# Hybrid S5 and attention block on one Trainium2 core: chunk outputs in pairs, Toeplitz blocks by way of DRAM

## Chip, cores and metric

One core of a Trainium2 chip runs the whole layer as one program. The metric is the device time in microseconds; before, it is 681.32 us (median of 3 runs, 681.21 to 681.42).

## What is computed

One decoder layer on 512 tokens of width 1024 in float32: RMSNorm, one input projection `h @ w_in` of 9216 columns, an S5 state-space branch, a dilated attention branch, gates, and an output projection. The change concerns the S5 branch. Cut to it, the reference is

```python
def chunk_step(carry, u_c):                       # u: 64 groups of 16 channels, 64 complex states each
    bu = einsum('blgp,gnp->blgn', u_c, bb)        # input to states (complex)
    h  = scan(h[t] = a * h[t-1] + bu[t])          # diagonal, per state
    y  = einsum('blgn,gpn->blgp', h_re, c_re) - einsum('blgn,gpn->blgp', h_im, c_im)
y = y + d_skip * u
g = gelu(y)
return g * sigmoid(g @ w_glu)
```

## The kernel before

Float32 accuracy comes from three passes in fp32r: each operand is split into a high and a low part (ACT writes the high part, DVE the low one: lines 234 and 236 for weights), and `mm3` (line 144) issues three matmuls of up to 512 columns. A projection unit of 128 output columns is 24 such matmuls, in the trace `pj`. Weights come through SP's queue into two raw tiles (line 220) and are converted two units ahead of their use.

The order of PE is written out by hand: every matmul and transpose is issued after the one before it (`issue_after`, lines 62 to 74). A running list of units (u, za, zs, v0, v, rs, ra; lines 886 to 889) is the filler, and `events` (lines 874 to 884) says before which group of six matmuls a piece of the S5 branch is put. One group is two k-steps of `mm3`, a unit of the filler four groups. The other engines' orders, and SP's, are picked by the framework's scheduler from a simulated timeline, subject to the data and to priorities that follow the program's order. `W0` = 16, `K0B` = 49, `V0B` = 74 and `Y0` = 88 are places in the count of groups.

The S5 branch takes time in steps of eight tokens (T = 8, 64 columns of steps), and has these pieces:

- `w_unit`, `x_unit` (lines 369 and 387): inputs to states for 8 groups, eight times, into `Xs`.
- the scan (lines 665 to 720) on DVE, in 11 portions put at every fourth group from W0+26. `tables_last` holds it behind the last coefficient operation traced so far (`coefs[0]`, line 356).
- `ca_load`, `ca_turn`, `ca_coef` (lines 736 to 766): for one of eight units j (8 groups of 16 channels each), C is loaded, turned on PE (`cps`), copied out by ACT into one of two scratch tiles `p3`, and multiplied with powers of A on DVE (12 operations, lines 354 to 356) into one of three buffers `ab[j % 3]`.
- `m_unit` (line 768): CA times B on PE (`kps`) gives the first block row of a Toeplitz matrix for each group; ACT copies 8 pieces of 16 rows to `kt`, POOL adds the diagonal of d_skip (`dg`), and POOL issues eight transfers from SBUF to SBUF (line 785), each shifted by 16 columns, into M, one of three buffers `Mb` that were zeroed once (`clear_m`).
- `y_unit` (line 788): M times inputs (`yps <- dd,uss`) plus CA times states (`yps <- ab,Xs`), 48 matmuls in the program and 96 in the trace; ACT copies to `ysb`.
- `g_unit` (line 814): `ysb` turned back on PE (`yT`), GELU on ACT and DVE, split into `gT_hi` and `gT_lo`, the inputs of the GLU matmuls that follow the filler.

`chunk(j)` (line 851) strings these together: turn of ysb j-1, turn of C for j+3, y of j, coefficients of j+3, M of j+2, loads of u for j+2 and of C for j+4. It is put at Y0 + (11 j + 1)//3, so at groups 88, 92, 95, 99, 103, 106, 110 and 114, and the last turn at 116. Three turns of C, at W0+16, W0+19 and W0+22, lie ahead of the scan; M for units 0 and 1 is made at K0B.

PSUM: projection tiles take banks 0 to 2 in turn, everything else (`bank`) banks 3 to 7 in turn. Tiles named `t2k` share six buffers.

## Time and profile before

| | before |
|---|---|
| median of 3 runs | 681.32 us |
| the profiled execution | 681.33 us |
| its span, first to last instruction | 679.3 us |
| PE, PEld busy | 671.1, 565.1 us |
| DVE, ACT, POOL busy | 465.5, 322.1, 119.9 us |
| SP's queue (hardware): packets, MB | 134872, 78.93 |
| POOL's queue (software): packets, MB | 2048, 2.36 |
| granted TensorE clock, mean | 0.999 |

Times in the views are microseconds from the start of the span. Groups of instructions are told by line, engine, operation and tiles (out <- in); line 69 and line 74 are the helpers through which all matmuls and transposes go, so PE is read by tile names. One row of a timeline is: start, duration, engine, line, operation, tiles, shapes, count, and in brackets how long the engine had been idle and what released it. A fp32 matmul shows as two instructions. In a list of waits the three numbers are: us in total, times, the longest. Matmuls are pipelined, so what one costs is read from start to start. The stretches of the chunks lie between 177 and 244 us.

### The profile page before, as it was taken

The page shows a single profiled execution, that of the slowest core. Times are in us where ns is not written, and L with a number is a line of the kernel's source. Part 1 is how long each engine was busy: PE and PEld are TensorE (multiplying, and loading weights), DVE is VectorE, ACT ScalarE, POOL GpSimd, SP SyncE. Part 2 cuts the span into 40 slices and gives each one's busy share as a digit, 9 for nine tenths or more (in the row PEclk, how much of TensorE's full clock was granted, in tenths as well). Part 3 has the DMA queues.
Part 4 walks back from the last instruction along what each step waited for, and adds up shares of the span by engine and source line. Part 5 has one row for each costly group of instructions (what it writes and reads, how often), then busy time and mean ns, then how long its engine had stood idle before and what let it go on. Part 6 is the DMA issues. An engine that isn't in the chain of part 4 may idle for free.

```text
span 679.3 us, 12710 instructions
## 1 busy us (share of the span) xinstructions
PE 671.1 (99%) x4826; PEld 565.1 (83%) x4826; DVE 465.5 (69%) x981; ACT 322.1 (47%) x675; POOL 119.9 (18%) x274
## 2 busy tenths in 40 slices
PE   8999999999999999999999999999999999999997
PEld 7988878889888888888889888888888888888886
DVE  7879879999788466653238777558675856667531
ACT  5454543423377664431244673556455745733210
POOL 1021000500255529610000030012001200120000
PEclk9999999999999999999999999999999999999999
DMA  9656524643556653563333422222322223237231
GB/s 293 122 140 166 130 70 114 173 144 108 154 117 158 154 155 117 182 202 108 94 93 94 140 63 83 58 79 63 94 67 74 78 63 94 94 131 288 94 124 62
DMA packets 137236, 82.13 MB, mean 121 GB/s; under 512 B 32720, under 2 KB 125656, under 8 KB 137048
## 3 DMA queue, kind: packets, MB, share of 16 engines
q1 hardware_dynamic: 134872, 78.93, 39.4%
q0 software_dynamic: 2048, 2.36, 2.2%
q8 instruction: 38, 0.62, 0.4%
q14 instruction: 22, 0.18, 0.1%
q10 hardware_dynamic: 256, 0.04, 0.0%
HBM read 68.46 MB, written 10.49 MB: 116 GB/s over the span
## 4 chain that ended last, share of the span: by engine, by line
PE 75%; issue 10%; DVE 6%; POOL 4%; ACT 2%; DMA 2%; SPq 0%; POOLq 0%; DVEq 0%; ACTq 0%
PE pj L69 63%; POOL dd L785 3%; PE sps L69 2%; PE ot L69 2%; PE ptp L74 2%; PE qtp L74 1%; DVE w_lo L236 1%; PE xps L69 1%; PE wps L74 1%; ACT w_hi L234 1%; DMA x_all<-in_x_dram 1%; DVE scn L686 1%; DMA dg<-in_d_skip_dram 1%; PE yps L69 1%; POOL kt L781 1%
## 5 line engine op out<-in xcount | busy, mean ns | idle before, releaser
L234 ACT ACTIVATE w_hi<-w_raw 128x1024 fp32r<-128x1024 f32 x96 | 101.7, 1060 | 170.8 <-PE pj L69 142.4
L236 DVE TENSOR_TENSOR w_lo<-w_raw,w_hi 128x1024 fp32r<-128x1024 f32 x96 | 120.2, 1253 | 76.0 <-ACT w_hi L234 75.4
L69 PE MATMUL pj<-hT_hi,w_hi 128*128 128x512 f32 (+1 forms) x344 | 131.8, 385 | 0.0
L69 PE MATMUL pj<-hT_lo,w_hi 128*128 128x512 f32 (+1 forms) x344 | 128.3, 376 | 0.0
L69 PE MATMUL pj<-hT_hi,w_lo 128*128 128x512 f32 (+1 forms) x344 | 126.6, 375 | 0.0
L69 PE MATMUL pj<-w_hi,hT_hi 128*128 128x512 f32 (+1 forms) x288 | 108.7, 377 | 0.0
L69 PE MATMUL pj<-w_hi,hT_lo 128*128 128x512 f32 (+1 forms) x288 | 105.6, 367 | 0.0
L69 PE MATMUL pj<-w_lo,hT_hi 128*128 128x512 f32 (+1 forms) x288 | 105.5, 366 | 0.0
L69 PEld LDWEIGHTS pj<-hT_hi,w_hi 128*128 128x128 f32 x344 | 64.7, 188 | 13.4 <-issue 1.3
L69 PEld LDWEIGHTS pj<-hT_hi,w_lo 128*128 128x128 f32 x344 | 63.7, 188 | 12.0
L69 PEld LDWEIGHTS pj<-hT_lo,w_hi 128*128 128x128 f32 x344 | 64.6, 188 | 10.7 <-DVE hT_lo L324 0.2
L69 PEld LDWEIGHTS pj<-w_hi,hT_lo 128*128 128x128 f32 x288 | 54.3, 189 | 9.1
L69 PEld LDWEIGHTS pj<-w_hi,hT_hi 128*128 128x128 f32 x288 | 54.4, 189 | 8.5 <-issue 0.5
L69 PEld LDWEIGHTS pj<-w_lo,hT_hi 128*128 128x128 f32 x288 | 54.5, 189 | 7.5
L1051 POOL COPY sw<-st 32x4 f32<-32x4 f32 x64 | 11.8, 185 | 174.4 <-ACT Pt L1007 171.5
L952 DVE SCALAR_TENSOR_TENSOR qkp<-qtp,wcol,qkp 128x512 fp32r<-128x512 f32 (+1 forms) x32 | 23.6, 748 | 25.3 <-ACT qkp L951 25.2
L1007 ACT ACTIVATE Pt<-Pt,st 128x256 f32<-128x256 f32 (+1 forms) x64 | 30.9, 484 | 19.3 <-DVE st L1005 19.3
L785 POOL DMA_DIRECT2D dd<-kt x64 | 33.7, 536 | 2.4 <-POOL kt L781 2.1
L951 ACT ACTIVATE qkp<-qtp,wcol 128x512 fp32r<-128x512 f32 (+1 forms) x32 | 21.2, 683 | 23.0 <-PE qtp L74 20.8
L69 PE MATMUL pj<-gT_hi,w_hi 128*128 128x512 f32 x64 | 25.0, 391 | 0.0
L69 PE MATMUL pj<-gT_hi,w_lo 128*128 128x512 f32 x64 | 24.9, 389 | 0.0
L69 PE MATMUL pj<-yT_hi,w_hi 128*128 128x512 f32 x64 | 24.9, 389 | 0.0
(296 smaller groups left out, 1182.7 us busy)
## 6 DMA issues: line engine op xcount, KB each, us to landing
w_raw<-in_w_in_dram SPq DMA_DIRECT2D x36, 512.0 KB
w_raw<-in_w_in_dram SPq DMA_DIRECT2D x112, 128.0 KB
w_raw<-in_w_glu_dram SPq DMA_DIRECT2D x8, 512.0 KB
w_raw<-in_w_ssm_out_dram SPq DMA_DIRECT2D x8, 512.0 KB
w_raw<-in_w_o_dram SPq DMA_DIRECT2D x8, 512.0 KB
x_all<-in_x_dram SPq DMA_DIRECT2D x4, 512.0 KB
w_early<-in_w_in_dram SPq DMA_DIRECT2D x4, 512.0 KB
ud<-uT SPq DMA_DIRECT2D x8, 256.0 KB
```

The costliest lines, as they stand in the source:

```text
L69: last[0] = nc.tensor.matmul(*a, **k)
L74: last[0] = nc.tensor.transpose(*a, **k)
L234: last_act[0] = act.activation(hi, raw, AF.Copy).ins
L236: dve.tensor_tensor(lo, raw, hi.bitcast(F32), op=ALU.subtract)
L686: dve.tensor_tensor(ta.rearrange("p o a (g j) -> p o (a g) j", j=NJ), prev.rearrange("p a g j -> p (a g) j").unsqueeze(1).broadcast_to(sh) ...
L781: pool.tensor_tensor(kt[:, :, T - 1, :], kt[:, :, T - 1, :], dg, op=ALU.add)
L785: pool.dma_start(M[Q * t:Q * t + Q, :, 0:P - Q * t], kt[:, :, t:].rearrange("q g k p -> q g (k p)"))
L951: act.activation(hi, ps[sl], AF.Copy, scale=w)
L952: dve.scalar_tensor_tensor(lo, ps[sl], w, hi.bitcast(F32), op0=ALU.mult, op1=ALU.subtract)
L1007: act.activation(o, o, AF.Exp, bias=nm, scale=-1.0, accum_out=st[:, kind, 1, h, b:b + 1])
L1051: pool.tensor_copy(sw[32 * r:32 * r + 32, :, :, b], st[32 * b:32 * b + 32, 1, :, :, r])
```

## The change

Chunk outputs are made for two units at a time: four stretches (`chunks(i)`, at Y0 + 7 i with Y0 = 91: groups 91, 98, 105, 112) and a last turn of two units at group 117. Four coefficient buffers (the fourth is a tile of its own, `cax`) hold units 0 to 3 ahead of the scan; C is turned in pairs, at W0+19 and W0+24. A pair of M is made from one set of two PSUM banks: `kps` takes 32 columns of B, of which the upper 16 are wanted, so that whole 128-row copies (two for a pair) bring it to `kt`; SP writes `kt` to the left half of rows in DRAM (`kd`), whose right half is zero, and reads M back with a stride that shifts by 16 columns for each of the eight blocks. `diagonals` prepares the masked d_skip for all units and the zeros of `kd` once.

```diff
-    W0, K0B, V0B, Y0 = 16, 49, 74, 88
+    W0, K0B, V0B, Y0 = 16, 49, 74, 91
...
+    kd = dram.tile([4, 2, P, 2, 2 * P], F32, name="kd")
+    def diagonals():
+        dv = d_skip[0].rearrange("(j m c) -> m j c", m=4, c=2 * Q)
+        for m in range(4):
+            sp.dma_start(dgs[32 * m:32 * m + 32].rearrange("q j h p -> q j (h p)"),
+                         dv[m:m + 1].to_broadcast([32, 8, 2 * Q]))
...
+        pool.tensor_tensor(flat, flat, dq, op=ALU.mult)
+        zt = t2k("zt")
+        pool.memset(zt[:, 0:P], 0.0)
+        for i in range(4):
+            for n in range(2):
+                sp.dma_start(kd[i, n, :, :, P:2 * P], zt[:, 0:P].unsqueeze(1).broadcast_to([P, 2, P]))
-    def ca_turn(j):
+    def ca_turn(*js):
         ps = bank("cps")
+        for n, j in enumerate(js):
...
-        ca = ab[j % 3].rearrange("p (a g k q) -> p a g k q", a=2, g=4, k=9)
+        ca = (ab[j % 4] if j % 4 < 3 else cax[0]).rearrange("p (a g k q) -> p a g k q", a=2, g=4, k=9)
-    def m_unit(j, ca, dg):
-        kt = big.tile([Q, 8, T, Q], F32, name="kt", tag=("s7a", "s7b")[j % 2])
...
-                act.copy(kt[:, 2 * m + h].rearrange("q k p -> q (k p)"), ps[h][32 * m:32 * m + Q, 0:P])
-        pool.tensor_tensor(kt[:, :, T - 1, :], kt[:, :, T - 1, :], dg, op=ALU.add)
-        M = Mb[j % 3]
-        for t in range(T):
-            pool.dma_start(M[Q * t:Q * t + Q, :, 0:P - Q * t], kt[:, :, t:].rearrange("q g k p -> q g (k p)"))
+    def make_m(i):
+        js = (2 * i, 2 * i + 1)
+        kt = big.tile([P, 2, 2, P], F32, name="kt", tag="s7b")
+        ps = [bank("kps") for _ in range(2)]
...
+                        pe.matmul(ps[h][32 * m:32 * m + 32, P * n:P * n + P], BBf[sl, o:o + 32],
+                                  cas[j][sl, c, m, 1:9, :], start=c == 0, stop=c == 1, skip_group_check=True,
+                                  tile_position=(64 * h, 32 * m))
+        for h in range(2):
+            act.copy(kt[:, :, h], ps[h][:, 0:2 * P].rearrange("r (n c) -> r n c", n=2))
...
+        for n, j in enumerate(js):
+            M = Mb[j % 3]
+            sp.dma_start(kd[i, n, :, :, 0:P], kt[:, n])
             for m in range(4):
+                rows = kd[i, n, 32 * m + Q:32 * m + 32].rearrange("q h c -> (q h) c")
+                (sr, nr), (sc, _) = rows.ap
+                shifted = bass.AP(rows.tensor, rows.offset, [(Q * sc, T), (sr, nr), (sc, P)])
+                sp.dma_start(M[:, 2 * m:2 * m + 2].rearrange("r g c -> r (g c)"), shifted)
...
+    def chunks(i):
+        js = (2 * i, 2 * i + 1)
+        turned = y_turn(i - 1) if i else []
+        if i < 2:
+            ca_turn(2 * i + 4, 2 * i + 5)
+        for j in js:
+            ysbs[j] = y_unit(j, cas[j], Ms.pop(j), Us.pop(j))
+        if i < 3:
+            make_m(i + 1)
+        for j in js:
+            if j + 4 < 8:
+                ca_coef(j + 4)
+        for j, s in turned:
+            gelu(j, s, *gTs)
+        for j in js:
+            if j + 2 < 8:
+                load_us(j + 2)
+            if j + 6 < 8:
+                ca_load(j + 6)
...
+    for j in range(4):
+        events += [(W0 + 12 + 3 * j, lambda j=j: ca_load(j)), (W0 + 25, lambda j=j: ca_coef(j))]
+    events += [(W0 + 19, lambda: ca_turn(0, 1)), (W0 + 24, lambda: ca_turn(2, 3)), (W0 + 24, states)]
+    events += [(W0 + 24, diagonals), (K0B, lambda: make_m(0)), (K0B, lambda: ca_load(4)), (K0B, lambda: ca_load(5))]
...
+    events += [(Y0 + 7 * i, lambda i=i: chunks(i)) for i in range(4)] + [(Y0 + 26, chunks_end)]
```

## The prediction

> **What bounds the kernel now.** I read the page first, for the busy shares and the chain that ended last.

> ```profile
> span 679.3 us, 12710 instructions
> PE 671.1 (99%) x4826; PEld 565.1 (83%) x4826; DVE 465.5 (69%) x981; ACT 322.1 (47%) x675; POOL 119.9 (18%) x274
> PE 75%; issue 10%; DVE 6%; POOL 4%; ACT 2%; DMA 2%; SPq 0%; POOLq 0%; DVEq 0%; ACTq 0%
> ```

> PE covers 99% of the span. The chain also walks through POOL (the transfers of line 785) and DVE for a while, but that says only which work was due at some point; whether PE ever stood still for it is said by the waits, taken for PE alone:

> ```profile
> PE nps L74 <- POOL dd L841: 2.9, 1, 2.9
> PE yps L69 <- DMA dd<-kt: 0.3, 1, 0.3
> ```

> 2.9 us is the start of the program, and 0.3 us is one wait for a Toeplitz block M. Everything else that the change touches (ACT's 16-row copies, POOL's descriptor work, the diagonals) is hidden behind PE already. So the change is worth what it takes from PE's own order, less every new wait of PE. Third view, the chain in order of time, for the price of PE's large matmuls in a long undisturbed run, and of transposes:

> ```profile
> 88.12 0.87 PE wps L74 x8
> 610.10 65.53 PE pj L69 x288
> ```

> A projection matmul (512 columns) costs 65.53/288 = 0.2275 us from start to start, a transpose 0.87/8 = 0.109 us.

> **What merging the stretches takes from PE.** In the timeline of PE, this is one chunk stretch of before (j = 1): transposes yT, coefficient turn cps, two kinds of yps, then kps and back to pj.

> ```profile
> 186.29 0.60 PE L74 MATMUL yT<-ident,ysb 128*128 128x128 f32 x4
> 186.82 0.45 PE L69 MATMUL cps<-ident,cn 128*64 128x64 f32 x8
> 187.10 1.10 PE L69 MATMUL yps<-dd,uss 128*64 128x64 f32 x32
> ...
> 189.23 0.65 PE L69 MATMUL kps<-ab,dd 64*16 64x128 f32 x32
> 189.81 0.50 PE L69 MATMUL pj<-hT_hi,w_hi 128*128 128x512 f32 x1
> ...
> 191.30 0.39 PE L69 MATMUL pj<-hT_hi,w_hi 128*128 128x512 f32 x1
> ```

> The last row is the seventh pj after the stretch. Six intervals take 191.30 - 189.81 = 1.49 us where 6 x 0.2275 = 1.365 would do: going back to full-size matmuls costs 0.13 us. Four transposes take 0.53 us up to cps, where 4 x 0.109 = 0.44 would do: 0.09 us more. So a stretch costs about 0.22 us beyond its work. The work itself is not reduced: cps, yps and kps keep their counts (kps now loads 32 columns of weights, but streams the same 128). Eight stretches become four: 4 x 0.22 = 0.88 us saved.

> The coefficient turns that stand alone ahead of the scan go from three to two. One of them:

> ```profile
> 91.27 0.40 PE L69 MATMUL pj<-hT_hi,w_lo 128*128 128x512 f32 x1
> 91.60 0.45 PE L69 MATMUL cps<-ident,cn 128*64 128x64 f32 x8
> ...
> 93.48 0.39 PE L69 MATMUL pj<-hT_hi,w_hi 128*128 128x512 f32 x1
> ```

> Between the first and last of these are seven pj intervals: 2.21 - 7 x 0.2275 = 0.62 us for one. A second turn in the same place adds its own work, 0.28 us (186.82 to 187.10). Three cost 1.86 us, two doubled ones 1.80: 0.06 us saved.

> The third item is two small stalls of before. One is the 0.3 us wait above. The other does not show as idle time:

> ```profile
> 219.98 0.60 PE L74 MATMUL yT<-ident,ysb 128*128 128x128 f32 x4
> 220.73 1.15 PE L69 MATMUL yps<-dd,uss 128*64 128x64 f32 x32
> ```

> 0.75 us where a turn takes 0.53: 0.22 us. Both are waits for an M that POOL's eight transfers brought late; if M now comes in time, 0.5 us goes. Sum: 0.88 + 0.06 + 0.5 = 1.44 us, and PE alone would give 681.33 (the profiled execution, with 2.03 us outside its span; the median of the runs is 681.32) - 1.44 = 679.9 us.

> **What the scan gives back.** The new order needs four coefficient buffers ahead of the scan instead of three, and `tables_last` queues the scan on DVE behind the last of them. These rows of DVE show coefficients, weight conversions and gates up to the start of the scan, its end, and the conversion just after it; below them all the idle time of DVE between 112.5 and 178 us, and the first matmuls on PE that need the scan.

> ```profile
> 103.16 1.42 DVE L354 TENSOR_TENSOR ab<-p,AT 128x576 f32<-128x576 f32 x2
> 109.07 0.76 DVE L356 TENSOR_TENSOR ab<-ab 128x576 f32<-128x576 f32 x1
> 110.97 1.23 DVE L236 TENSOR_TENSOR w_lo<-w_raw,w_hi 128x1024 fp32r<-128x1024 f32 x1 [0.35 <-ACT w_hi L234]
> 112.12 0.75 DVE L356 TENSOR_TENSOR ab<-ab 128x576 f32<-128x576 f32 x1
> 112.78 0.69 DVE L666 COPY scn<-A 128x1024 f32<-128x1024 f32 x1
> 113.69 0.68 DVE L570 SCALAR_TENSOR_TENSOR z<-th,pj 128x512 f32<-128x512 f32 x1
> 114.29 1.22 DVE L686 TENSOR_TENSOR scn<-Xs,scn 128x1024 f32<-128x1024 f32 x1
> 177.09 0.69 DVE L691 TENSOR_TENSOR Xs<-Xs,scn 128x512 f32<-128x512 f32 x1
> 178.68 1.23 DVE L236 TENSOR_TENSOR w_lo<-w_raw,w_hi 128x1024 fp32r<-128x1024 f32 x1 [0.89 <-ACT w_hi L234]
> ```

> ```profile
> DVE w_lo L236 <- ACT w_hi L234: 1.7, 5, 0.6
> ```

> ```profile
> 179.02 1.16 PE L69 MATMUL yps<-ab,Xs 64*64 64x64 f32 x64
> ```

> The scan ends at 177.09 + 0.69 = 177.78 and PE needs it at 179.02: 1.24 us of room. Eight coefficient operations start between 103.16 and 109.07, so one costs 0.74 us, a buffer of six 4.4 us, a pair 8.9 us. After the change buffers 2 and 3 hang on the second double turn, at block W0+24. That block begins where the conversion at 110.97 belongs, and 0.96 us earlier (two single turns gone, one doubled: 2 x 0.62 - 0.28). Two scratch tiles hold the turned coefficients, so buffers 0 and 1 must be done by then: they begin at the first double turn, five groups of six pj (6.8 us) and the x stretches between ahead of it, which about holds their 8.9 us with one conversion and one gate (what were left over would come on top). The conversion then runs from 110.0 to 111.2 (110.97 to 112.12 is 1.15 us), and the second pair behind it, with one more conversion (1.15) and two gates (0.60 each, 113.69 to 114.29) falling into it: 111.2 + 8.9 + 1.15 + 1.2 = 122.4. Before, the scan began at 112.78 with those 2.35 us still ahead of it. The scan is late by 122.4 - 112.8 - 2.35 = 7.3 us. DVE's waits for ACT, 1.7 us, go when DVE is itself late; the conversion at 178.68 now falls ahead of the end of the scan, 1.15 us. End of scan: 177.8 + 7.3 - 1.7 + 1.15 = 184.5. PE gets there three groups of six matmuls later (Y0 88 to 91, 18 x 0.2275 = 4.1 us), 0.06 earlier by the turns and 0.28 later by the doubled cps: 179.0 + 4.1 - 0.06 + 0.28 = 183.3. So PE waits about 1.2 us at the first stretch. Ends: 0, if the second pair starts 1 us sooner, or the operations follow each other faster where two buffers are interleaved; 3 us, if the waits for ACT stay. I take the worked value; it is lost on PE in full, since nothing else is queued there. Forecast: 679.9 + 1.2 = 681.1, which I round to 681.0.

> **The new way of M.** Before, POOL issued eight transfers from SBUF to SBUF per unit; now SP writes kt to DRAM and, when that has landed, reads it back four times with a shift. SP also issues all weights, so a wait there holds them; and M now hangs on SP's order. Nearest rows: a copy of 256 columns out of PSUM, the add on POOL, SP's wait for a write to DRAM that it reads back (ud), its issue time for 256 KB, the landing of the old M.

> ```profile
> L811 ACT COPY ysb<-yps 128x256 f32<-128x256 f32 x16 | 5.1, 368 | 0.8 <-PE yps L69 0.8
> L781 POOL TENSOR_TENSOR kt<-kt,dg 16x128 f32<-16x128 f32 x8 | 5.4, 672 | 99.1 <-ACT kt L780 99.1
> ```

> ```profile
> SPq L341 <- DMA ud<-uT: 11.3, 4, 5.1
> ```

> ```profile
> L341 SPq DMA_DIRECT2D uss<-ud x8: 594/606/1257, 109.0 to 222.5; - x8
> ```

> ```profile
> DMA to landing us min/median/max: 1.7/3.3/6.2
> ```

> From the end of kps: two copies 0.74, add 0.67, write issued 0.6 and awaited 2.8 (11.3/4), four reads issued 2.4, landed 3.3: 10.5 us. PE's window from there to the next yps is 42 x 0.2275 + 0.13 + eight transposes 0.87 + 0.09 = 10.65 us, 0.28 more where cps stands between, and 2.1 us more for the second unit of the pair (187.10 to 189.23), whose reads follow the first's by 2.4. So M comes just in time: cost nothing, cover 0.2 us. With the longest wait for DRAM (5.1) it is 2.1 us late, in each of three stretches (the first pair is made 42 groups ahead). For weights SP's wait is covered: they are converted two units ahead of their use.

> [...]

> **At no cost.** The copies from PSUM fall from 16 to 2 for a pair and POOL loses its descriptor work; neither is on PE's path, so neither gains. The zeroed right half of kd and the diagonals are issued at block W0+24, nine groups of six matmuls (12 us) ahead of the first M that needs them. The last turn now does two units 18 matmuls ahead of the GLU instead of one unit 24 ahead. Cover:

> ```profile
> 243.25 0.60 PE L74 MATMUL yT<-ident,ysb 128*128 128x128 f32 x4
> 249.55 0.68 DVE L123 SCALAR_TENSOR_TENSOR gT_lo<-gq,gT_hi 128x512 fp32r<-128x512 f32 x1
> ```

> One unit is through 7.0 us after its turn began; a second adds about three DVE steps of 0.7, 9.1 us. It is needed at the eighth weight block: 0.96 + 0.13 + (18 + 22) x 0.2275 = 10.2 us. 1.1 us to spare; without it, up to 1 us.

> **Rivals.** *The scan is in time* (against: 1.24 us of room before; for: DVE idles between coefficients, and the order may close these gaps). Then PE's saving stands: 679.9 us, 679.4 to 680.3. It decides at a scan end of 183.3. *M is late* (for: the wait of up to 5.1 us on SP, and a window with 0.2 us to spare; against: 2.8 us on average, and SP is free to put write, write, reads in a row). It is slower than before: 2.1 us in each of three stretches is 6.3 us, so 681.0 to 687.3, and half of that, 684.2 us, as its price. It decides when write plus reads take 0.2 us over 10.5. That ACT and POOL become free can bring nothing beyond the first rival, since PE waits for neither.

> **How the numbers follow.** This kernel can be told from no change at about 0.2%, 1.4 us: 680.0 to 682.7. Scan late by 0.3 to 3 us, M in time: 0.40, 680.2 to 682.9, nearly all of it "same". Scan in time: 0.35, of which some three quarters lie under 680.0, since the saving (1.44) is hardly over the bound. M late: 0.25, nearly all slower. Faster 0.27, same 0.46, slower 0.27. The likeliest case's range is 680.2 to 682.9; for 8 in 10 I add the faster case down to 679.3 and M's up to 685.3, which leaves out a few in a hundred below and the upper third of M late.

> **What would show it.** Right: four chunk stretches of about 7 us on PE, a wait of PE at yps <- ab,Xs for DVE L691 of about 1 us in the first, none at yps <- dd; scan end near 184.5; waits of SP for kd of 2 to 3 us. Wrong: no wait for the scan (then DVE's coefficients were done before 120); PE waits for dd <- kd; any wait at the first gT matmuls; or a stretch that costs more than two of before, because kps or yps meet a PSUM bank that ACT has not emptied.

## The result, and the profile after

The changed kernel takes 697.28 us (median of 4 runs, 693.39 to 698.32) beside 681.35 us before (681.21 to 681.42): 1.0218 times, with a 95% interval of 1.0202 to 1.0234. It is slower by 15.9 us, outside my range. The profiled execution took 697.05 us. First its page: span, busy times, the chain that ended last, and the row of the queue that brings instructions.

```profile
span 695.3 us, 12583 instructions
PE 677.7 (97%) x4826; PEld 571.8 (82%) x4826; DVE 464.7 (67%) x981; ACT 310.5 (45%) x619; POOL 75.8 (11%) x200
q8 instruction: 38, 0.62, 0.4%
PE 87%; DVE 5%; ACT 3%; DMA 2%; issue 1%; SPq 1%; POOL 0%; POOLq 0%; ACTq 0%; DVEq 0%
```

PE's share fell from 99% to 97% although it does the same 4826 rows, and its busy time rose by 6.6 us. So PE both stands still and runs slower somewhere. Its waits say where it stands (us in total, times, longest):

```profile
PE yps L69 <- DVE Xs L691: 3.9, 1, 3.9
PE kps L69 <- issue: 2.4, 1, 2.4
PE pj L69 <- DVE gT_lo L123: 2.0, 1, 2.0
PE yps L69 <- issue: 1.2, 1, 1.2
PE yps L69 <- DMA dd<-kd: 0.3, 1, 0.3
```

Two of these I had priced: the scan (3.9 in place of 1.2) and M (0.3 in place of 0). "issue" means that no semaphore ended the wait. Where it stood is seen in PE's timeline, here the second stretch:

```profile
204.46 1.04 PE L74 MATMUL yT<-ident,ysb 128*128 128x128 f32 x8
205.43 0.69 PE L69 MATMUL cps<-ident,cn 128*64 128x64 f32 x16
205.94 1.10 PE L69 MATMUL yps<-dd,uss 128*64 128x64 f32 x32
...
209.15 1.16 PE L69 MATMUL yps<-ca,Xs 64*64 64x64 f32 x64
210.24 0.66 PE L69 MATMUL kps<-ab,dd 64*32 64x128 f32 x29
213.32 0.93 PE L69 MATMUL kps<-ab,dd 64*32 64x128 f32 x35 [2.42 <-issue]
214.18 0.79 PE L69 MATMUL pj<-hT_hi,w_hi 128*128 128x512 f32 x1
214.78 0.63 PE L69 MATMUL pj<-hT_lo,w_hi 128*128 128x512 f32 x1
```

PE stops after row 29 of 64 in kps, in the middle of one run of alike matmuls. Behind the stop a projection lasts 0.63 us, not 0.39. That is the other part: the granted clock. Stretches of time around the wait for the scan, the stop in kps and the wait for gT_lo (us; busy PE, PEld, DVE, ACT, POOL; PEclk; DMA share; GB/s):

```profile
183.20:186.60 3.40, 1.07 (x38) 0.93 (x32) 3.33 (x5) 0.68 (x4) 0.00 (x0) 1.00 0.37 96
186.60:193.40 6.80, 5.27 (x150) 5.04 (x153) 4.77 (x8) 0.65 (x2) 0.00 (x0) 0.50 0.20 46
...
210.60:214.00 3.40, 0.98 (x56) 0.60 (x40) 3.26 (x6) 1.46 (x4) 0.00 (x0) 0.99 0.65 160
214.00:217.40 3.40, 3.40 (x11) 2.54 (x9) 3.40 (x6) 1.80 (x4) 0.50 (x1) 0.50 0.35 92
217.40:220.80 3.40, 3.40 (x16) 2.77 (x15) 2.33 (x4) 2.31 (x4) 0.00 (x0) 1.00 0.40 111
...
265.20:268.60 3.40, 1.36 (x5) 0.78 (x5) 3.33 (x7) 0.00 (x0) 1.15 (x1) 1.00 0.00 0
268.60:272.00 3.40, 3.40 (x9) 2.63 (x8) 1.99 (x5) 2.95 (x5) 2.68 (x9) 0.50 0.76 236
```

After a stop of 2.42 us and one of 2.04 us the clock is 0.50 for 3.4 us; after the wait for the scan it is so for 6.8 us (186.6 to 193.5). Priced by PE's starts: 2.3 us behind the scan (188.13 to 193.71, where e1 below takes 3.26 us for the same rows), 1.5 us behind the stop in kps (42 projections in 11.17 us in place of 9.68), 1.7 us behind the wait for gT_lo (14 projections in 5.0 us in place of 3.3).

The account at the first matmul of the norm weights (`wcp`, 257.4 us before, 273.3 after): scan 3.85, stops 2.42 + 1.19, M 0.34, gT_lo 2.04, half clock 2.3 + 1.5 + 1.7, and 0.9 of a later start (the first `ftp` at 44.7 in place of 43.8; in the runs below, whose start is the same code, it lies between 43.8 and 44.5, so this is mostly chance). That is 16.2, but most of it in idle times. Counted from start to start, as the prediction counts, the scan and its half clock take 6.2, the stops 2.9 and 1.5, M 0.7 and the wait for gT_lo 2.2; with the other half clocks (1.5 and 1.7) and the later start this is 17.6. The shift is 15.8. So the forecast saving of 1.4 is there (about 1.8 by this count), under the losses. From there to the end the shift stays.

### The profile page after: what moved, and what is told of

It reads as the page before. It is cut to its first block, busy times and chain, and to the rows that moved or that the text cites. A ratio compares the mean times of both kernels' runs of the same rounds, so it can differ in the third digit from the quotient of the medians.

```text
span 695.3 us, 12583 instructions
## 1 busy us (share of the span) xinstructions
PE 677.7 (97%) x4826; PEld 571.8 (82%) x4826; DVE 464.7 (67%) x981; ACT 310.5 (45%) x619; POOL 75.8 (11%) x200
## 4 chain that ended last, share of the span: by engine, by line
PE 87%; DVE 5%; ACT 3%; DMA 2%; issue 1%; SPq 1%; POOL 0%; POOLq 0%; ACTq 0%; DVEq 0%
PE pj L69 72%; PE yps L69 2%; PE sps L69 2%; PE ot L69 2%; PE ptp L74 2%; DVE w_lo L236 2%; PE qtp L74 1%; PE xps L69 1%; PE warm L74 1%; ACT w_hi L234 1%; PE wps L74 1%; DMA dd<-kd 1%; DMA rope<-in_positions_dram 1%; DVE qkp L992 1%; SPq L815 1%
## 5 line engine op out<-in xcount | busy, mean ns | idle before, releaser
L234 ACT ACTIVATE w_hi<-w_raw 128x1024 fp32r<-128x1024 f32 x96 | 101.6, 1060 | 180.7 <-PE pj L69 138.9
L236 DVE TENSOR_TENSOR w_lo<-w_raw,w_hi 128x1024 fp32r<-128x1024 f32 x96 | 120.9, 1260 | 77.9 <-ACT w_hi L234 73.0
L69 PE MATMUL pj<-hT_hi,w_hi 128*128 128x512 f32 (+1 forms) x344 | 132.0, 386 | 0.0
L69 PE MATMUL pj<-hT_lo,w_hi 128*128 128x512 f32 (+1 forms) x344 | 128.8, 378 | 0.0
L69 PE MATMUL pj<-hT_hi,w_lo 128*128 128x512 f32 (+1 forms) x344 | 127.0, 377 | 0.0
L69 PE MATMUL pj<-w_hi,hT_hi 128*128 128x512 f32 (+1 forms) x288 | 108.7, 377 | 0.0
L69 PE MATMUL pj<-w_hi,hT_lo 128*128 128x512 f32 (+1 forms) x288 | 105.6, 367 | 0.0
L69 PE MATMUL pj<-w_lo,hT_hi 128*128 128x512 f32 (+1 forms) x288 | 105.5, 366 | 0.0
L69 PEld LDWEIGHTS pj<-hT_hi,w_hi 128*128 128x128 f32 x344 | 65.1, 189 | 13.0 <-issue 0.9
L69 PEld LDWEIGHTS pj<-hT_lo,w_hi 128*128 128x128 f32 x344 | 65.0, 190 | 10.9 <-DVE hT_lo L324 0.2
L69 PEld LDWEIGHTS pj<-hT_hi,w_lo 128*128 128x128 f32 x344 | 64.0, 189 | 12.1
L69 PEld LDWEIGHTS pj<-w_hi,hT_lo 128*128 128x128 f32 x288 | 54.3, 189 | 9.1
L69 PEld LDWEIGHTS pj<-w_hi,hT_hi 128*128 128x128 f32 x288 | 54.4, 189 | 8.5 <-issue 0.5
L69 PEld LDWEIGHTS pj<-w_lo,hT_hi 128*128 128x128 f32 x288 | 54.5, 189 | 7.5
L69 PE MATMUL pj<-gT_lo,w_hi 128*128 128x512 f32 x64 | 25.7, 401 | 2.0 <-DVE gT_lo L123 2.0
L69 PE MATMUL pj<-gT_hi,w_hi 128*128 128x512 f32 x64 | 25.7, 401 | 0.0
L69 PE MATMUL pj<-gT_hi,w_lo 128*128 128x512 f32 x64 | 25.6, 401 | 0.0
L69 PE MATMUL pj<-yT_hi,w_hi 128*128 128x512 f32 x64 | 24.9, 389 | 0.0
```

Of the source, the lines that this page charges most:

```text
L69: last[0] = nc.tensor.matmul(*a, **k)
L234: last_act[0] = act.activation(hi, raw, AF.Copy).ins
L236: dve.tensor_tensor(lo, raw, hi.bitcast(F32), op=ALU.subtract)
```

## The experiments

My theory after the result had four parts: **(1)** the late second turn makes the scan late; **(2)** PE runs out of instructions in the doubled stretches; **(3)** the GELU of the last two units meets other DVE work; **(4)** stops of some 2 us halve the clock. Rivals: the stops of (2) come from PSUM banks, ACT or SP's loads; SP's zero writes make the scan late; M by DRAM is the true loss.

**Turns earlier (e1).** The changed kernel with

```diff
-    events += [(W0 + 19, lambda: ca_turn(0, 1)), (W0 + 24, lambda: ca_turn(2, 3)), ...
+    events += [(W0 + 16, lambda: ca_turn(0, 1)), (W0 + 22, lambda: ca_turn(2, 3)), ...
```

and the loads of C at W0 + 6, 9, 18, 21.

> The changed kernel with one part undone: the two double turns of C at W0+16 and W0+22 in place of W0+19 and W0+24 (loads of C to match). In the changed kernel DVE stands 4.47 us at 94.7 to 99.8 for the first turned coefficients, and PE then waits 3.85 us for the scan and runs the next 5.6 us at about half clock, which costs another 2.3 us. Theory A (the late turns alone make the scan late): DVE's gap goes, the scan ends 4 to 5 us earlier, PE's wait for DVE Xs falls under 0.5 us, the granted clock of 180 to 200 us returns to 0.95 or more, and the time is 690.5 to 692.5 us. Rival B (the weights held up on SP behind the zero writes make the scan late): PE still waits 2 us or more and the time is 694 to 697 us. The two PE stalls of 2.4 and 1.2 us in the second and third stretch, which no semaphore ended, stay in both.

692.08 us (691.28 to 693.86; 1.0152 of before, 1.0130 to 1.0173). The wait is gone, and so is the half clock behind it, in PE's timeline:

```profile
182.76 1.10 PE L69 MATMUL yps<-dd,uss 128*64 128x64 f32 x32
183.80 1.16 PE L69 MATMUL yps<-ab,Xs 64*64 64x64 f32 x64
184.89 1.15 PE L69 MATMUL yps<-dd,uss 128*64 128x64 f32 x32
```

The two stops stayed, 2.0 and 2.4 us. Theory (1) holds; the zero writes on SP were as before, so that rival falls.

**The instruction stream shifted (e2).** The page's q8 row gives 0.62 MB in 38 packets, and the trace shows each as 16384 bytes. PE's recorded instructions in the whole program are 9745, about 38 times 256 (9728). Between the two stops (211.5 to 230.8 us) the trace records 255 weight loads, 255 matmuls and 2 semaphore instructions: 512, exactly twice 256. So I added 64 rows of unused matmuls long before the stretches:

```diff
+    events += [(K0B + 8, lambda: dense(7, 7, 6, 6, 6))]
```

> The changed kernel with 64 more rows of PE work (32 small fp32 matmuls into a scratch bank, result unused) at group K0B+8, long before the stretches. Theory A (PE runs out of instructions: between the two stalls that no semaphore ended stand exactly 512 of PE's recorded instructions, and the instruction queue brings 16384 bytes at a time): every place where PE can run dry moves 128 instructions, 64 rows, earlier in the program. In the second stretch the stall leaves row 29 of kps and comes at row 29 of the second yps of the states; in the third it leaves row 42 of the second yps of the states and comes at row 42 of kps; in the fourth, which had none, one appears near row 54 of its second yps of the states. Length 1 to 3 us each. Rival B (a PSUM bank that ACT has not emptied, or the loads on SP's queue): the stalls stay at the same rows, kps 29 and yps 42. Rival C (chance of DMA traffic): no order in where they fall. Time within 3 us of the changed kernel's.

PE's timeline in the second and fourth stretch:

```profile
206.40 0.68 PE L69 MATMUL yps<-ca,Xs 64*64 64x64 f32 x29
208.12 0.80 PE L69 MATMUL yps<-ca,Xs 64*64 64x64 f32 x35 [1.04 <-issue]
...
243.52 1.04 PE L69 MATMUL yps<-ca,Xs 64*64 64x64 f32 x54
244.75 0.39 PE L69 MATMUL yps<-ca,Xs 64*64 64x64 f32 x10 [0.19 <-issue]
```

Row 29 and row 54, as worked out beforehand; in the third stretch no stop over 0.2 us came, though one was due at kps row 42. The places belong to the instruction stream and not to a bank, an engine or a transfer. Of the lengths only 1.04 lay in the 1 to 3 us expected, 0.19 below. The time was 690.86 us (one run), 6.4 less than the changed kernel's and not within 3 us of it: here PE reached the scan later, so that wait was gone, but M was now waited for five times, 2.3 us in all.

**Dense runs alone (e4, e7).** The kernel before, with unused dense matmuls put among its projections.

> The kernel before with four dense runs of small fp32 matmuls (64 by 64, result unused) put among its projections at K0B+6, +14, +22 and +30, where neither scan nor chunks use PE: 160, 280, 280 and 640 rows, each row a weight load and a matmul of about 17 ns. No data is waited for. Theory A (a block of 256 instructions, 128 rows, lasts 2.2 us, and the next is there about 4.1 us after PE enters the block before it): no stall or one under 1 us in 160 rows; one stall of about 1 to 2.5 us in each run of 280; four stalls of 1 to 3 us in 640 rows, 128 rows apart, so that run takes 17 to 20 us in place of 10.9. After stalls of 2 us or more the projections run at about 0.43 us in place of 0.2275 for some us. Rival B (the stalls come from PSUM banks, ACT or SP's loads in the chunk stretches): no stall that no semaphore ended, 640 rows in 11 us.

This missed its aim: all rows wrote one place, and a row took 58 ns, a block of 128 rows 7.4 us. No stop, 762.69 us (one run): it says only that blocks run this slowly came in time. Again with halves and output places taken in turn:

```diff
+                m, f, h = k // 4 % 4, k // 2 % 2, k % 2
+                pe.matmul(ps[h][64 - 64 * f:128 - 64 * f, 64 * m:64 * m + 64], BBp[sl, 0:64], BBp[sl, 64:128], ...
```

> The dense runs again (160, 280 or more, and 640 rows among the projections of the kernel before, result unused), now with the two halves of the contraction and the output places taken in turn as the y stretches do, so that a row lasts about 17 ns and not 57: 160, 320, 320 and 640 rows. Theory A (instructions come in blocks of 256, that is 128 rows, 2.2 us; the next is there some 4 to 5.5 us after PE entered the block before): at most one small stall in 160 rows, one or two of 1 to 2.5 us in 320, four in 640, 128 rows apart; the 640 rows take 17 to 22 us in place of 11. Rival B (the stalls of the chunk stretches come from banks, ACT or SP's loads): no stall that no semaphore ended; 640 rows in 11 us.

PE's timeline in the run of 640 rows, and the row of the instruction queue from 183 to 199 us:

```profile
183.39 3.60 PE L69 MATMUL prb<-dd 64*64 64x64 f32 x231
188.03 2.09 PE L69 MATMUL prb<-dd 64*64 64x64 f32 x128 [1.03 <-issue]
191.48 2.09 PE L69 MATMUL prb<-dd 64*64 64x64 f32 x128 [1.36 <-issue]
194.93 2.09 PE L69 MATMUL prb<-dd 64*64 64x64 f32 x128 [1.36 <-issue]
198.66 0.58 PE L69 MATMUL prb<-dd 64*64 64x64 f32 x25 [1.64 <-issue]
```

```profile
q8 instruction: 4, 0.07, 1.6%
```

Runs of exactly 128 rows, with nothing to wait for: a block takes 2.09 us to run, and blocks follow at 3.45 us (3.73 for the last). The run of 160 rows had no stop, those of 320 one each (1.43 and 0.90). The 640 rows took 15.9 us, a little less than the 17 to 22 expected (the kernel 717.47 us, one run). Theory (2) is shown. A row is two instructions, so the 128 rows between two stops are the 256 counted in e2.

The packets themselves are in the traces, and they settle it. In the changed kernel one came from 211.11 to 212.06 us, inside the stop that ended at 213.32. In all runs together there are 18 stops without a semaphore, and each ended 1.2 to 1.6 us after the end of a packet on q8 (the two of the changed kernel 1.27 and 1.35 us). How long a stop was went with when the packet started. Counting 256 instructions from a stop gives the other borders. In the 640 rows of e7 a packet started 1.1 us after PE entered the block before (188.03 and 189.15). In the changed kernel it was 3.2 us (207.87 and 211.11), with the DMA engines 93% busy in between. In the first stretch of e1 it was 0.2 us (183.80 and 184.01), and PE crossed two borders in one dense piece of 272 rows without a stop. So 3.45 us is the pace of e7 and not a fixed time; what sets the start of a packet stays open.

The kernel before is exposed too: in e7 and in e8 below, which are that kernel with instructions added, PE stopped 2.0 and 1.6 us in kps of a single stretch (132 rows: yT, yps and kps of one unit). Before has no such stop; that its borders fall elsewhere would explain it.

**The rope behind GELU (e3).** The DVE order of the changed kernel explains the 2.04 us wait for gT_lo:

```profile
261.85 0.17 DVE L1181 CAST rope<-rope 128x4 f32<-128x4 int32 x1 [1.49 <-DMA rope<-in_positions_dram]
262.03 0.26 DVE L1193 TENSOR_SCALAR qkw<-qkw 128x192 f32<-128x192 f32 x1
262.21 0.69 DVE L860 SCALAR_TENSOR_TENSOR gq<-gq,gs 128x512 f32<-128x512 f32 x1
262.81 1.79 DVE L1184 TENSOR_SCALAR rope<-rope 128x4 f32<-128x4 f32 x8
264.51 0.68 DVE L123 SCALAR_TENSOR_TENSOR gT_lo<-gq,gT_hi 128x512 fp32r<-128x512 f32 x1
265.11 1.28 DVE L441 TENSOR_SCALAR rope<-rope 128x32 f32<-128x32 f32 x1
266.31 1.21 DVE L236 TENSOR_TENSOR w_lo<-w_raw,w_hi 128x1024 fp32r<-128x1024 f32 x1
267.44 0.17 DVE L442 TENSOR_SCALAR rope<-rope 128x32 f32<-128x32 f32 x1
267.53 0.68 DVE L123 SCALAR_TENSOR_TENSOR gT_lo<-gq,gT_hi 128x512 fp32r<-128x512 f32 x1
```

DVE waited 1.49 us for the positions with half-done GELU behind it. So, with `splits[0]` the last gT_lo, and the same for the first operation on the norm weights (line 1193):

```diff
-    dve.tensor_copy(pos_f, pos_i)
+    with tc.issue_after(splits[0]):
+        dve.tensor_copy(pos_f, pos_i)
```

> The changed kernel with DVE's rope angles and norm weights (lines 1181 to 1193 of the changed kernel) held behind the last gT_lo. In the changed kernel PE waits 2.04 us for gT_lo at 266.2 and runs at about half clock for 3.7 us after it, 1.8 us more. Theory A (DVE stood behind a load of positions that SP issued late): the wait for gT_lo falls under 0.4 us, the clock of 260 to 280 us is 0.98 or more, the time 693 to 694.5 us. Rival B (a second unit of GELU so close to the GLU matmuls is too much for DVE and ACT in itself): PE still waits 1 us or more for gT_lo and the time is 695.5 us or more.

691.38 us (688.81 to 693.70; 1.0139, 1.0109 to 1.0168). No wait for gT_lo is left. The median is some 2 us below the range expected, and the runs spread over 4.9 us. The two profiled executions are 5.0 us apart (697.05 and 692.03): from start to start 3.9 is the wait for gT_lo and its half clock, 0.7 that M was not late in this run, and most of the rest two slightly shorter stops (1.60 and 1.77 us, only the second followed by half clock) and an earlier start.

**Pauses (e8).** The kernel before with six pauses of PE, made by

```diff
+    events += [(K0B + 3 + 6 * k, lambda n=n: pause(n)) for k, n in enumerate((0, 1, 2, 3, 5, 8))]
```

> The kernel before with six pauses of PE among its projections, from K0B+3 at every sixth group: a small matmul, a copy on ACT, 0, 1, 2, 3, 5 and 8 copies on POOL, and a matmul that waits for the last (result unused). Theory A (the granted clock falls to half by the length of the pause alone, at a length between 1.2 and 2.0 us): after pauses up to about 1.5 us the projections run at 0.23 us, after those of 2 us or more at about 0.43 us for 3 to 6 us, which costs 1.5 to 2.5 us beside the pause. Rival B (the half clock in the changed kernel goes with the dense stretches, not with the pause): all projections at 0.23 us after every pause.

The kernel took 707.31 us (one run). The pauses came out at 1.38, 1.29, 3.83, 1.50, 3.41 and 2.70 us. Windows before and after the pause of 3.83 us, and around that of 2.70:

```profile
147.50:150.90 3.40, 1.31 (x7) 0.74 (x5) 3.37 (x8) 1.63 (x3) 0.84 (x1) 1.00 0.00 0
150.90:157.70 6.80, 5.06 (x13) 3.97 (x14) 6.73 (x9) 0.00 (x0) 1.63 (x2) 0.50 0.38 120
...
188.40:191.80 3.40, 2.23 (x11) 1.50 (x9) 1.23 (x1) 1.02 (x2) 0.69 (x3) 1.00 0.03 7
191.80:195.20 3.40, 1.88 (x9) 1.55 (x10) 0.00 (x0) 0.00 (x0) 1.16 (x6) 1.00 0.50 147
```

3.83 and 3.41 halved the clock; the four others did not, 2.70 among them, while 1.77 us did in e3. Length alone, my theory, does not decide. The changes of clock in one trace lie on a grid of 3.41 us (in the changed kernel 193.5, 214.0, 217.4, 268.6, 272.0). The pause of 2.70 us is split over two slots, in which PE was busy 2.23 and 1.88 us of 3.4; the stop in e3 lay in one slot with 1.63 us busy. That stop's slot and the next, in e3:

```profile
227.30:230.70 3.40, 1.63 (x87) 1.42 (x94) 0.00 (x0) 0.17 (x1) 0.00 (x0) 1.00 0.91 267
230.70:234.10 3.40, 3.40 (x69) 2.63 (x47) 2.17 (x4) 3.40 (x9) 0.32 (x1) 0.51 0.57 128
```

The other stop of e3 was nearly as long, 1.60 us, but its slot had 1.80 us busy, and the clock stayed. What fits nearly all rows is the busy time of the slot. Slots at full clock with 0.98, 1.07 and 1.36 us busy (changed kernel) and 1.31 us (e8) were followed by half clock; those with 1.80 us (e3) and with 1.88 and 2.23 us (e8) were not. Between, both occur: 1.63 us in e3 was followed by half clock, 1.51 us in e9 below (232.7 to 236.1) was not, so the border is not sharp in this measure. In the changed kernel, e3 and e8 full clock came back only after a slot in which PE was busy throughout (3.40 of 3.40 us, as from 214.0 in the changed kernel and from 230.7 in e3); in the changed kernel the slot from 186.6 to 190.0, itself at half clock and 1.9 us busy, was followed by another at half clock.

**M by DRAM alone (e6).** The kernel before, eight stretches, with only the new way of M, unit by unit:

```diff
-        for t in range(T):
-            pool.dma_start(M[Q * t:Q * t + Q, :, 0:P - Q * t], kt[:, :, t:].rearrange("q g k p -> q g (k p)"))
+        sp.dma_start(kd[j // 2, j % 2, :, :, 0:P], kt)
+        for m in range(4):
...
+            sp.dma_start(M[:, 2 * m:2 * m + 2].rearrange("r g c -> r (g c)"), shifted)
```

> The kernel before with M's way by DRAM alone: eight stretches, three coefficient buffers and single turns as before; kps with 32 columns of B, two 128-row copies, the diagonal added from one prepared table, one write and four shifted reads on SP for each unit, zeros written once. Theory A (the way by DRAM is in time when M is made two stretches ahead, some 10 us): no wait for dd, 680.8 us, within 0.2% of before. Rival B (SP's write and reads are too slow): PE waits for dd 0.5 us or more in several stretches, 683 us or more.

690.97 us (689.71 to 692.25; 1.0137, 1.0117 to 1.0156). Rival B: my theory was wrong here. One wait line of PE and one of SP:

```profile
PE yps L69 <- DMA dd<-kd: 5.1, 10, 1.0
```

```profile
SPq L807 <- DMA kd<-kt: 16.4, 7, 3.2
```

On SP the write waits its turn behind the reads of the M before it, gates, weights and inputs (the one for the kps at 206.6 us was issued at 212.0), then the reads wait 2.3 us on average for the write. In the changed kernel this way was late by only 0.34 us. A likely reason, not tested by itself, is that PE had already been held up by other things: in e2, where the stops were shorter, M was late by 2.3 us.

**All repaired (e5, e9, e10, e11).** M still by DRAM and C in pairs; with e1 and e3, and each double stretch cut up. e5: kps two groups ahead of the first y, the second y two groups behind it.

```diff
+    events += [(Y0 + 7 * i - 2, lambda i=i: kps_ahead(i + 1)) for i in range(3)]
+    events += [(Y0 + 7 * i + 2, lambda i=i: second(i)) for i in range(4)]
```

> The changed kernel with all that was found undone at once, M still by way of DRAM and C still turned in pairs: turns at W0+16 and W0+22; rope angles behind the last gT_lo; and each double stretch cut into three dense pieces with two groups of projections between them: kps two groups ahead (64 rows), then the turn of y and the first y (104 rows), two groups later C and the second y (112 rows). Theory A (all of the loss is the scan, the instruction blocks that come too late, the end chain, and the half clock behind the long ones): 697.3 less 3.9 + 2.3 (scan and its clock), 2.4 + 1.2 + 1.5 (stalls and clock), 0.3 (M) and 2.0 + 1.8 (end), plus eight more returns to projections at 0.22 us, so 683.6 us, 682.5 to 685; clock 0.998 or more; no stall without a semaphore over 0.5 us. Rival B (dense stretches are not the cause; the stalls come with ACT, the banks or SP's loads): stalls of 1 us or more remain, 686 us or more. Rival C: with the stalls gone M is late instead, PE waits for dd 1 us or more in some stretch, 685 to 688 us.

690.02 us (689.71 to 692.46; 1.0134, 1.0114 to 1.0154), above the 682.5 to 685 expected. No stop without a semaphore, no wait for the scan, M or gT_lo. But kps now came too early for its coefficients, a wait that I had made myself, with 6.8 us at half clock behind it:

```profile
PE kps L69 <- DVE ab L358: 3.4, 4, 1.1
PE kps L69 <- DVE ca L358: 2.0, 2, 1.1
```

e9 turns C with kps, one group ahead, and begins the coefficients right behind the first y.

```diff
-    events += [(Y0 + 7 * i - 2, lambda i=i: kps_ahead(i + 1)) for i in range(3)]
+    events += [(Y0 + 7 * i - 1, lambda i=i: kps_ahead(i + 1)) for i in range(3)]
...
     def kps_ahead(i):
+        if i < 3:
+            ca_turn(2 * i + 2, 2 * i + 3)
         make_m(i)
```

> The version with all repaired, where PE still waited 5.4 us in kps for the coefficients on DVE and lost some more to half clock: now C is turned together with kps, one group (not two) ahead of each pair's first y, and the coefficients of the first unit are begun right behind the first y, some 4 us sooner; kps comes one group later. Theory A (the 5.4 us and their clock were all that was left of the loss): kps waits under 1 us in all, M stays in time, clock 0.999; the time is that of the kernel before plus four more returns to projections (0.9 us) less the 0.5 us of its M waits: 682.1 us, 681 to 684. Rival B (DVE has no room for the coefficients of a pair between two pairs): kps still waits 2 us or more, 685 us or more. Rival C (a loss that is not seen as waits, for instance slower projections beside the traffic to DRAM): no waits over 0.5 us and still 685 us or more.

685.57 us (683.37 to 689.33; 1.0061, 1.0039 to 1.0083), again above the range expected. Those waits fell to 0.7 us, but a third took their place, since on SP the eight reads of M stood ahead of the inputs:

```profile
PE yps L69 <- DMA uss<-ud: 3.6, 2, 3.3
```

e10 puts them in the other order:

```diff
+            with tc.issue_after(load_us(j + 2)):
+                read_m(j + 2)
```

> The last version with one more edit: on SP's queue each load of inputs (uss) goes ahead of the four shifted reads of M, not behind all eight. There PE waited 3.6 us for uss in two places and 0.7 us in kps, and nothing else was left. Theory A (that is all of the rest): PE's waits in the stretches fall under 1 us in sum, the clock is 0.999, and the time is that of the kernel before plus four more returns to projections (0.9 us) less the 0.5 us of its M waits: 682.1 us, 681 to 683.5. Rival B (SP and the DMA rings have no room for M's write and reads beside the weights): the wait only changes its name, to dd <- kd or w_hi, and the time stays above 684.5 us.

682.14 us (11 runs, 682.02 to 682.98; 1.0011, 1.0002 to 1.0021). The waits and the clock are as theory A has them; that the time agrees to the tenth is luck. There are eleven dense pieces, three more than before and not four as I wrote, and a wait of 0.8 us in kps is left. With 681.39 us before, 0.66 more, 0.5 less and this 0.8 the sum would be 682.3. What the change lost is back to 0.1%. Last, e11 moves kps up to the first y: eight pieces.

```diff
-    events += [(Y0 + 7 * i - 1, lambda i=i: kps_ahead(i + 1)) for i in range(3)]
+    events += [(Y0 + 7 * i, lambda i=i: kps_ahead(i + 1)) for i in range(3)]
```

> The last version with kps and the turn of C moved up to each pair's first y, so that the four pairs come in eight dense pieces (up to 184 rows) in place of eleven. Theory A (a return to projections costs 0.22 us; PE runs dry where two block borders, 128 rows apart, lie in one dense piece): 3 returns less is 0.66 us, so 681.5 us where no stall comes. By the places of the borders in the changed kernel the first pair has one at its kps and one 128 rows on, at the end of its first piece: a stall of 1 to 2 us there and none in the other pairs, 682.5 to 683.5 us. Rival B (borders do not matter, only the 280 rows of a full stretch): no stall, 681.5 us. Rival C (the shorter time for M): a wait for dd of 1 us or more, 683 us or more.

681.77 us (11 runs, 680.75 to 682.17; 0.9997, 0.9988 to 1.0006): no different from before, and below the 682.5 to 683.5 expected. The stop of the first pair came at the worked place, the end of its first piece, but of 0.2 us; one of 0.4 us came where I had none. Borders are placed well by counting; the length of a stop is not. No version beats the kernel before.

## Why the prediction was wrong, step by step

**What merging saves.** The step "The work itself is not reduced ... Eight stretches become four: 4 x 0.22 = 0.88 us saved" failed in what it put at nothing. The saving itself is there by the starts. But the step priced a stretch by its matmuls at the pace of one stretch of 140 rows and left out the supply of instructions. A stretch of 280 rows crosses two borders of 128 rows, whose rows are run in some 2.1 us, and in two of the four stretches the next block came later than that. Cost: 2.42 + 1.19 us idle (4.4 from start to start) and 1.5 us of clock. I had listed "a stretch that costs more than two of before" as a way to be wrong, but gave it a PSUM bank as its cause and no price.

**The scan.** The mechanism was right (a wait at yps for DVE Xs in the first stretch) and the size off: 3.85 us in place of 1.2. The term is the second pair of coefficients, which I let end at 122.4; the scan began at 126.8. DVE's timeline after:

```profile
117.26 1.23 DVE L236 TENSOR_TENSOR w_lo<-w_raw,w_hi 128x1024 fp32r<-128x1024 f32 x1 [0.47 <-ACT w_hi L234]
...
124.38 1.22 DVE L236 TENSOR_TENSOR w_lo<-w_raw,w_hi 128x1024 fp32r<-128x1024 f32 x1 [1.58 <-ACT w_hi L234]
...
126.79 0.68 DVE L666 COPY scn<-A 128x1024 f32<-128x1024 f32 x1
```

The pair began at 112.7 and not at 111.2, two conversions fell into it and not one, and the waits for ACT, which I let go "when DVE is itself late", grew: 0.47 and 1.58 us here. (A unit takes six coefficient operations, as this sum has it, not the twelve that the section on the kernel before gives.) The upper end of 3 us, "if the waits for ACT stay", was the better guess. That the first pair would be done by 110 held (110.1).

**The clock.** No step had it. Each wait was priced at its length, and three of them cost 5.5 us more than that.

**M.** "M comes just in time" held by the trace, 0.34 us late once. But it held by luck: alone, the way by DRAM costs 9.3 us (e6). The rival's mechanism was right; "half of that" of 2.1 us a stretch was too little for SP's order.

**The last double turn.** "1.1 us to spare" failed by 3.1 us: 2.04 us of wait. I counted GELU's own three DVE steps and not the rope angles, which DVE's order puts between them (e3).

**The sign.** I forecast no change with equal chances to both sides. Places at which the change took away spare room gave way together, DVE ahead of the scan, DVE ahead of the GLU and a little SP's queue; I had let them go one at a time. The supply of instructions and the clock I had not listed at all.

## What to carry to other kernels

Count the instructions of a dense run of small matmuls: at 17 ns a row, some dense runs of 132 to 640 rows between long stretches of large matmuls had stops of 0.2 to 2.4 us here that no semaphore shows, and 64 rows elsewhere moved them (e2). Price a wait of PE by how long it leaves PE busy in a clock slot of 3.41 us (up to 1.36 us was followed by half clock here, 1.80 us or more was not), not by its length alone. Before merging work into fewer, larger pieces, list what else stands in each queue (SP's loads, DVE's conversions) in the time that the piece now needs at once.
